# The weight block of the fourth leading unit's second product, loaded and rounded before the sums of unit 0

## The chip, the cores and the metric

The kernel runs on one core of one Trainium2 chip. The metric is the device time of one execution in microseconds (us). Times here are the median of several executions; the profile is one further execution, taken by the hardware profiler.

The engines are PE (TensorE: matrix products), ACT (ScalarE), DVE (VectorE), POOL (GpSimd, which here mainly issues adding transfers) and SP (SyncE, which issues plain transfers). Each has an instruction stream of its own and waits on semaphores for the others.

## What is computed

A trunk of two layers over 512 tokens of width 1024 in float32. Each layer is a token mixer and a SwiGLU channel mixer, each followed by a residual sum and a layer norm:

```python
for i in range(DEPTH):                      # DEPTH = 2
    m = diff_attention(h, ...) if i % 2 == 0 else short_gated_conv(h, ...)
    h = layer_norm(ALPHA * h + m, ln1_g[i], ln1_b[i])
    h = layer_norm(ALPHA * h + swiglu(h, w_gate[i], w_up[i], w_down[i]), ln2_g[i], ln2_b[i])

def swiglu(x, w_gate, w_up, w_down):        # w_gate, w_up: 1024 x 2816; w_down: 2816 x 1024
    return (silu(x @ w_gate) * (x @ w_up)) @ w_down
```

The change lies in the gate and up products of SwiGLU, once in each layer.

## The kernel before

**Precision.** PE multiplies float32 values in a rounded form (F32R). Every factor is therefore split into a rounded `hi` and a rest `lo`, and a product is three matmuls: hi·hi, hi·lo, lo·hi. The split of a plain weight block is `plain` (line 171): two ACT instructions write `hi` (L173) and the negated copy `lo` (L174), and then POOL issues a transfer that adds the raw block onto `lo` (L175). The split of a computed value is `split` (L57 on ACT for `hi`, then L58 on DVE for `lo`).

**Units and blocks.** The 2816 hidden columns fall into 11 units of 256. For each unit the gate and the up weights are cut into 2x2 blocks named "11", "12", "21", "22" (512 KB each). A unit is computed as seven block products in the manner of Strassen and Winograd, on sums of weight blocks (`t1` to `t4`, L611 on DVE) and on sums of activation blocks (`s1` to `s4`). The products of one unit in order are: x11 with block 11 (`start`), x12 with block 21 (`second`, into the same bank `x`), then `rest`: s2 with t2 into a bank `y`, s1 with t1 into a bank `z`, s3 with t3 added onto `y`, s4 with block 22 added onto `z`, and x22 with t4 added onto `y`. One product is 24 matmuls of 128x128 weights and 256 columns, all on line 623. Before `y` is added to, DVE must have read it (`u2`, L663); before `z` is added to, DVE must have read it (`w5`, L667).

**Leading units.** At the start of each SwiGLU the activations of tokens 256 to 511 are not ready. So the first four units (LEAD = 4) do their `start` and `second` products first; these need only tokens 0 to 255. Meanwhile ACT and DVE form s1 to s4 and x22 for the other tokens (`turn_forms`, lines 231 to 243) in two pieces, `soon` and `later`. `next21(u)` loads block 21 of unit u and splits it by `plain`. `sums(0, ...)` computes t1 and t2 of unit 0.

**Buffers.** Blocks 11 and 22, and block 21 of the leading units, go through three buffers tagged `raw`; blocks 12 and 21 of the rest go through two buffers tagged `raw2`. Blocks 12 and 22 of unit 0 are loaded into these two by hand. Block 21 of unit 0, called `raw_0_21` below, therefore waits until `t3` has read block 12; and block 12 of unit 1, `raw_1_12`, waits until `t4` has read `raw_0_21`. On SP the load of `raw_0_21` stands behind that of block 11 of unit 2, which waits for the adding transfer of the fourth leading unit's block 21.

**Order.** The recording layer orders each engine's instructions by the position in the program and by a plan of its own for when operands are ready; an engine then runs its stream strictly in that order. ACT's stream is therefore not the order of the source lines.

Of the kernel before, what the change touches and what calls it, by code (L numbers as in the profile page):

```python
# [39 lines left out]
def trunk(ctx: ExitStack, tc: tile.TileContext, t: dict):  # L40
# [4 lines left out]
    wpool = ctx.enter_context(tc.tile_pool(name="wpool", bufs=6))  # L45
# [4 lines left out]
    def bank(name):  # L50
        return psum.tile([P, 512], F32, tag="ps", name=name)
# [49 lines left out]
    def slot(pool, tag, shape, dt, name):  # L101
        return pool.tile([P, *shape], dt, tag=tag, name=name)
# [56 lines left out]
    def load_gu(i, u, key, pool, tag, n):  # L159
        a, b = int(key[0]) - 1, int(key[1]) - 1  # L160
        raw = pool.tile([P, 4, 256], F32, tag=tag, name=f"raw_gu{i}_{u}_{key}", bufs=n)
        nc.sync.dma_start(raw, t["wgu"][i, u, a, b])
        return raw

    def pair_gu(name):
        hi = wpool.tile([P, 4, 256], F32R, tag="whi", name=f"whi_{name}")
        lo = wpool.tile([P, 4, 256], F32R, tag="wlo", name=f"wlo_{name}")
        return hi, lo


    def plain(raw, name, pair=None):
        hi, lo = pair or pair_gu(name)
        nc.scalar.copy(hi, raw)  # L173
        nc.scalar.activation(lo, raw, AF.Copy, scale=-1.0)  # L174
        nc.gpsimd.dma_start(lo, raw, accum_op=ALU.add)  # L175
        return hi, lo
# [14 lines left out]
    lead = {}  # L191
# [399 lines left out]
    def swiglu(i, x, turns, open_next, out):  # L591
# [3 lines left out]
        with ExitStack() as fctx:  # L595
            wk = fctx.enter_context(tc.tile_pool(name=f"gu{i}", bufs=1, reuse_waits="tile"))

            def blocks(u, keys):
                return {
                    key: load_gu(i, u, key, *((wpool, "raw", 3) if key[0] == key[1] else (wk, "raw2", 2)))  # L600
                    for key in keys
                }

            def combined(raw, name):
                hi, lo = pair_gu(name)
                split(hi, lo, raw)
                return hi, lo
# [7 lines left out]
            def product(ps, w, key, first):  # L615
                xh, xl = x[key]
                for f in range(2):
                    o = ps[:, f * HALF : (f + 1) * HALF]
                    fs = slice(f * P, (f + 1) * P)
                    for k in range(4):  # L620
                        wh, wl = w[0][:, k, fs], w[1][:, k, fs]
                        for n, (a, b) in enumerate(((wh, xh), (wh, xl), (wl, xh))):
                            nc.tensor.matmul(o, a, b[:, k, :], start=first and f + k + n == 0,  # L623
                                             stop=k == 3 and n == 2, skip_group_check=True)

            def temp(tag, u, bufs=1):
                return wk.tile([P, 512], F32, tag=tag, name=f"{tag}{i}_{u}", bufs=bufs)
# [5 lines left out]
            def start(u, w):  # L633
                s = {"x": bank(f"x{i}_{u}")}
                product(s["x"], w, "x11", True)
                if u < 3:
                    both = slot(slots["xa"], f"h{UNITS - 5 - u}", (2, 512), F32, f"lead{i}_{u}")
                    s["e"], s["g"] = both[:, 0, :], both[:, 1, :]
                else:
                    s["e"], s["g"] = temp("e", u, 2), temp("g", u)  # L640
                return s

            def keep(s):
                nc.scalar.copy(s["e"], s["x"])
# [5 lines left out]
            def sums(u, raw):  # L650
                nm = f"gu{i}_{u}_"
                t1 = tsum(raw["12"], raw["11"], ALU.subtract, nm + "t1")
                t2 = tsum(raw["22"], t1, ALU.subtract, nm + "t2")
                return t1, t2, combined(t2, nm + "t2")
# [33 lines left out]
            def next21(u):  # L688
                return plain(load_gu(i, u, "21", wpool, "raw", 3), f"gu{i}_{u}_21")

            state, w2, later = [], [], []
            state.append(start(0, lead[i][0]))
            w2.append(next21(0))
            keep(state[0])
            soon = turns[0]()
            w2.append(next21(1))
# [1 line left out]
            later.append(soon[1])  # L698
            state.append(start(1, lead[i][1]))
            keep(state[1])  # L700
            soon = turns[1]()
            for u in range(2, LEAD):
                state.append(start(u, lead[i][u]))
            soon[0]()
            later.append(soon[1])
            raw = load_gu(i, 2, "21", wpool, "raw", 3)
            raw0 = {key: load_gu(i, 0, key, wk, "raw2", 2) for key in ("12", "22")}
            raw0.update(blocks(0, ("11",)))
            keep(state[2])
            w2.append(plain(raw, f"gu{i}_2_21"))  # L710
            keep(state[3])
            tw = sums(0, raw0)
            w2.append(next21(3))
            t1w = combined(tw[0], f"gu{i}_0_t1")
            for f in later:
                f()
# [4 lines left out]
            for u in range(1, UNITS):  # L721
                raw = blocks(u, ("11", "12", "22", "21"))
# [27 lines left out]
    def open_conv():  # L750
        slots["c"] = right_pool("x2")
        return new_xT(slots["c"], "x2")

    xT2, turns = swiglu(0, xT1, turns, open_conv, None)


    with ExitStack() as cctx:
# [42 lines left out]
        for ct in range(2, KD):  # L800
# [9 lines left out]
                             fetch=lambda: fetch_gu(1))  # L810

    swiglu(1, xT3, turns, lambda: None, t["out"])
    slots.pop("f").release()

# [51 lines left out]
```

## Time and profile before

| What | Value |
|---|---|
| Executions without profile | 1133.21, 1133.42, 1137.79 us |
| Median | 1133.42 us |
| The profiled execution | 1137.3 us |
| Span in its trace, first to last instruction | 1135.5 us (1.8 us lie around it) |
| PE busy | 1113.9 us, 98% |
| DVE busy | 736.3 us, 65% |
| ACT busy | 522.1 us, 46% |
| POOL busy | 118.6 us, 10% |
| Mean granted TensorE clock | 0.997 of full |
| HBM traffic | 119.81 MB read, 2.10 MB written |

PE carries the time: it is busy for all but some 22 us of the span, so a change of other engines' work shows in the time where PE waits, or comes to wait. The stretches of the change are the beginnings of the two SwiGLU blocks, near 250 to 290 us and 780 to 820 us. The three runs without profile spread over 4.6 us, and the profiled execution stands at the upper end of that spread.

### The profile page before, as it was taken

How to read it: one execution, taken by the hardware profiler on the slowest of the kernel's cores; microseconds unless marked ns; L12 is line 12 of the kernel's file. 1: busy time of each engine (PE TensorE's matmuls, PEld its weight loads, DVE VectorE, ACT ScalarE, POOL GpSimd, SP SyncE). 2: the span in 40 equal slices, each digit the busy share in tenths (PEclk: the TensorE clock that was granted, in tenths of full speed). 3: DMA queues.
4: the chain of work that ended last, by engine and by line, in shares of the span. 5: the costliest groups of instructions: out<-in, count | busy, mean ns of one | idle time of the engine just before them, and what ended most of it. 6: DMA issues, size and time to landing. Idle time of an engine off the chain costs nothing.

```text
span 1135.5 us, 17877 instructions
## 1 busy us (share of the span) xinstructions
PE 1113.9 (98%) x7242; PEld 994.1 (88%) x7242; DVE 736.3 (65%) x1065; ACT 522.1 (46%) x790; POOL 118.6 (10%) x149
## 2 busy tenths in 40 slices
PE   9999999999999999999999999999899999999997
PEld 6877887788999999988889888889899999988886
DVE  6777877587996776823355544448798767672416
ACT  5555555656455565711212432235555565651210
POOL 1111112140011111000010000013001111100002
PEclk9999999999999999999999999999999999999999
DMA  8521212278678777533313433377777877753302
GB/s 271 199 77 38 75 57 83 68 171 244 195 189 191 191 176 186 133 109 93 111 56 112 148 93 93 96 182 168 205 195 198 183 178 185 158 149 93 110 21 74
DMA packets 45315, 157.68 MB, mean 139 GB/s; under 512 B 5264, under 2 KB 6160, under 8 KB 45232
## 3 DMA queue, kind: packets, MB, share of 16 engines
q1 hardware_dynamic: 35728, 121.93, 34.7%
q0 software_dynamic: 9504, 34.61, 16.8%
q8 instruction: 57, 0.93, 0.3%
q14 instruction: 26, 0.21, 0.1%
HBM read 119.81 MB, written 2.10 MB: 107 GB/s over the span
## 4 chain that ended last, share of the span: by engine, by line
PE 73%; DVE 11%; DMA 5%; issue 4%; ACT 4%; POOL 2%; SPq 0%; POOLq 0%; DVEq 0%; ACTq 0%
PE y L623 14%; PE z L623 9%; PE x L623 7%; PE o_dn L77 7%; PE o_dn L76 7%; PE o_dn L75 7%; PE in L75 4%; PE in L77 4%; PE in L76 4%; DMA raw_gu<-in_wgu 3%; DMA wlo_gu<-raw_gu 2%; ACT p L476 1%; DVE nm L473 1%; DVE gu_t L611 1%; PE o_wo L75 1%
## 5 line engine op out<-in xcount | busy, mean ns | idle before, releaser
L57 ACT CAST whi_gu_t<-gu_t 128x1024 fp32r<-128x1024 f32 x88 | 91.1, 1049 | 82.0 <-DVE gu_t L611 40.5
L58 DVE TENSOR_TENSOR wlo_gu_t<-gu_t,whi_gu_t 128x1024 fp32r<-128x1024 f32 x88 | 107.1, 1223 | 30.0 <-ACT whi_gu_t L57 30.0
L58 DVE TENSOR_TENSOR wlo_dn<-raw_dn,whi_dn 128x1024 fp32r<-128x1024 f32 x44 | 53.6, 1223 | 112.5 <-ACT whi_dn L57 112.4
L75 PE MATMUL o_dn<-whi_dn,hid 128*128 128x512 f32 (+1 forms) x320 | 123.8, 387 | 0.0
L77 PE MATMUL o_dn<-whi_dn,hid 128*128 128x512 f32 (+1 forms) x320 | 123.8, 387 | 0.0
L76 PE MATMUL o_dn<-wlo_dn,hid 128*128 128x512 f32 (+1 forms) x320 | 123.8, 387 | 0.0
L57 ACT CAST whi_dn<-raw_dn 128x1024 fp32r<-128x1024 f32 x44 | 46.1, 1052 | 141.0 <-PE o_dn L77 107.5
L623 PE MATMUL x<-x_x_hi,wlo_gu 128*128 128x256 f32 x352 | 99.3, 282 | 4.3 <-DMA wlo_gu<-raw_gu 4.3
L175 POOL DMA_DIRECT2D wlo_gu<-raw_gu x66 | 57.5, 871 | 437.1 <-ACT wlo_gu L174 368.8
L623 PE MATMUL y<-x_s_hi,whi_gu_t 128*128 128x256 f32 x352 | 98.9, 281 | 1.3 <-DVE u L663 1.3
L623 PE MATMUL x<-x_x_hi,whi_gu 128*128 128x256 f32 x352 | 99.4, 282 | 0.0
L623 PE MATMUL x<-x_x_lo,whi_gu 128*128 128x256 f32 x352 | 98.9, 281 | 0.0
L623 PE MATMUL y<-x_s_hi,wlo_gu_t 128*128 128x256 f32 x352 | 98.3, 279 | 0.0
L623 PE MATMUL y<-x_s_lo,whi_gu_t 128*128 128x256 f32 x352 | 98.2, 279 | 0.0
L173 ACT CAST whi_gu<-raw_gu 128x1024 fp32r<-128x1024 f32 x66 | 69.0, 1050 | 61.3 <-PE y L623 30.7
L75 PE MATMUL in<-x_hi,whi_in 128*128 128x512 f32 (+1 forms) x240 | 83.7, 349 | 0.0
L77 PE MATMUL in<-x_hi,wlo_in 128*128 128x512 f32 (+1 forms) x240 | 83.2, 347 | 0.0
L76 PE MATMUL in<-x_lo,whi_in 128*128 128x512 f32 (+1 forms) x240 | 82.8, 345 | 0.0
L174 ACT ACTIVATE wlo_gu<-raw_gu 128x1024 fp32r<-128x1024 f32 x66 | 69.7, 1055 | 7.5 <-PE o_wco L76 6.0
L76 PEld LDWEIGHTS o_dn<-wlo_dn,hid 128*128 128x128 f32 x320 | 60.2, 188 | 13.1
L77 PEld LDWEIGHTS o_dn<-whi_dn,hid 128*128 128x128 f32 x320 | 60.1, 188 | 13.0
L75 PEld LDWEIGHTS o_dn<-whi_dn,hid 128*128 128x128 f32 x320 | 60.2, 188 | 13.0
(237 smaller groups left out, 3115.8 us busy)
## 6 DMA issues: line engine op xcount, KB each, us to landing
raw_gu<-in_wgu SPq DMA_DIRECT2D x104, 512.0 KB, 4.6
wlo_gu<-raw_gu POOLq DMA_DIRECT2D x66, 512.0 KB, 5.9
raw_dn<-in_wdn SPq DMA_DIRECT2D x44, 512.0 KB, 3.6
raw_in<-in_win SPq DMA_DIRECT2D x24, 512.0 KB, 3.6
raw_qk<-in_wqk SPq DMA_DIRECT2D x14, 512.0 KB, 3.9
raw_v<-in_wv SPq DMA_DIRECT2D x8, 512.0 KB, 5.5
raw_wo<-in_wo SPq DMA_DIRECT2D x8, 512.0 KB, 3.6
raw_wco<-in_wco SPq DMA_DIRECT2D x8, 512.0 KB, 3.8
```

The lines of the kernel that those rows point to most:

```text
L57: nc.scalar.copy(hi, src)
L58: nc.vector.tensor_tensor(lo, src, hi.bitcast(F32), op=ALU.subtract)
L75: nc.tensor.matmul(out, lh, rh, start=first, stop=False)
L76: nc.tensor.matmul(out, lh, rl, start=False, stop=False)
L77: nc.tensor.matmul(out, ll, rh, start=False, stop=last)
L173: nc.scalar.copy(hi, raw)
L174: nc.scalar.activation(lo, raw, AF.Copy, scale=-1.0)
L175: nc.gpsimd.dma_start(lo, raw, accum_op=ALU.add)
L473: nc.vector.tensor_reduce(nm, ps[c][:, :n], axis=AX.X, op=ALU.max, negate=True)
L476: nc.scalar.activation(pc[:, :n], ps[c][:, :n], AF.Exp, bias=nm, accum_out=sm)
L611: nc.vector.tensor_tensor(r, a, b, op=op)
L623: nc.tensor.matmul(o, a, b[:, k, :], start=first and f + k + n == 0, stop=k == 3 and n == 2, skip_group_check=True)
```

## The change

Block 21 of the fourth leading unit (u = 3) is loaded and split by `plain` in the place where that of the third (u = 2) stood, ahead of `sums(0, ...)`; before, it stood behind it. The block of the third unit moves up to just behind `keep(state[1])`. The number of instructions, loads and bytes stays the same.

```diff
-            state, w2, later = [], [], []
-            state.append(start(0, lead[i][0]))
-            w2.append(next21(0))
+            state, later = [start(0, lead[i][0])], []
+            w2 = [next21(0)]
...
             state.append(start(1, lead[i][1]))
             keep(state[1])
+            w2.append(next21(2))
             soon = turns[1]()
             for u in range(2, LEAD):
                 state.append(start(u, lead[i][u]))
             soon[0]()
             later.append(soon[1])
-            raw = load_gu(i, 2, "21", wpool, "raw", 3)
             raw0 = {key: load_gu(i, 0, key, wk, "raw2", 2) for key in ("12", "22")}
             raw0.update(blocks(0, ("11",)))
+            raw = load_gu(i, 3, "21", wpool, "raw", 3)
             keep(state[2])
-            w2.append(plain(raw, f"gu{i}_2_21"))
+            w2.append(plain(raw, f"gu{i}_3_21"))
             keep(state[3])
             tw = sums(0, raw0)
-            w2.append(next21(3))
             t1w = combined(tw[0], f"gu{i}_0_t1")
```

The order of instructions on PE, on POOL and on SP is the same in both kernels, apart from buffer numbers. What moves is on ACT and DVE.

ACT, first layer, from the rounding of s2 for tokens 256 to 383 on. In the names, `gu0_3_21` is block 21 of the fourth unit, `gu0_0_t2` the sum t2 of unit 0, `x1_s1` to `x1_s4` and `x1_x22` the activation sums, `lead0_2` and `e0_3` the kept partial products. Before:

```order
L57 CAST x1_s2_hi_2679<-x1_raw_x11_2685 128x4x128
L57 CAST x1_s3_hi_2681<-x1_raw_s3_2688 128x4x128
L57 CAST x1_s1_hi_2675<-x1_raw_x21_2687 128x4x128
L57 CAST x1_x22_hi_2677<-tp_wo_3_1_3027 128x4x128
L644 COPY lead0_2_3057<-x0_2_3032 128x512
L57 CAST whi_gu0_0_t2_3112<-gu0_0_t2_3110 128x1024
L57 CAST x1_s2_hi_2679<-x1_raw_x11_2685 128x4x128
L173 CAST whi_gu0_3_21_3118<-raw_gu0_3_21_3116 128x1024
L644 COPY e0_3_3083<-x0_3_3058 128x512
L174 ACTIVATE wlo_gu0_3_21_3119<-raw_gu0_3_21_3116 128x1024
L57 CAST whi_gu0_0_t1_3123<-gu0_0_t1_3108 128x1024
```

After the change, from the same instruction on:

```order
L57 CAST x1_s2_hi_2679<-x1_raw_x11_2685 128x4x128
L173 CAST whi_gu0_3_21_3109<-raw_gu0_3_21_3106 128x1024
L174 ACTIVATE wlo_gu0_3_21_3110<-raw_gu0_3_21_3106 128x1024
L57 CAST x1_s1_hi_2675<-x1_raw_x21_2687 128x4x128
L644 COPY lead0_2_3064<-x0_2_3039 128x512
L57 CAST whi_gu0_0_t2_3119<-gu0_0_t2_3117 128x1024
L57 CAST x1_s2_hi_2679<-x1_raw_x11_2685 128x4x128
L57 CAST whi_gu0_0_t1_3123<-gu0_0_t1_3115 128x1024
L644 COPY e0_3_3090<-x0_3_3065 128x512
L57 CAST x1_s3_hi_2681<-x1_raw_s3_2688 128x4x128
L57 CAST x1_x22_hi_2677<-tp_wo_3_1_3034 128x4x128
```

The two instructions of `gu0_3_21` move up past the roundings of s3, s1, x22, s2 and t2.

DVE, first layer, from the sum behind t2 (s2 for tokens 384 to 511) to t3. Before:

```order
L234 TENSOR_TENSOR x1_raw_x11_2685<-x1_raw_x21_2687,x1_raw_x11_2685 128x4x128
L58 TENSOR_TENSOR x1_s1_lo_2676<-x1_raw_x21_2687,x1_s1_hi_2675 128x4x128
L58 TENSOR_TENSOR x1_s3_lo_2682<-x1_raw_s3_2688,x1_s3_hi_2681 128x4x128
L58 TENSOR_TENSOR wlo_gu0_0_t2_3113<-gu0_0_t2_3110,whi_gu0_0_t2_3112 128x1024
...
L58 TENSOR_TENSOR x1_s4_lo_2684<-x1_raw_x12_2686,x1_s4_hi_2683 128x4x128
L58 TENSOR_TENSOR x1_x22_lo_2678<-tp_wo_3_1_3027,x1_x22_hi_2677 128x4x128
L241 TENSOR_TENSOR x1_raw_x12_2686<-x1_raw_x12_2686,x1_raw_x11_2685 128x4x128
L611 TENSOR_TENSOR gu0_0_t3_3297<-raw_gu0_0_22_3097,raw_gu0_0_12_3095 128x1024
```

After the change, the same stretch:

```order
L234 TENSOR_TENSOR x1_raw_x11_2685<-x1_raw_x21_2687,x1_raw_x11_2685 128x4x128
L58 TENSOR_TENSOR x1_s1_lo_2676<-x1_raw_x21_2687,x1_s1_hi_2675 128x4x128
L58 TENSOR_TENSOR wlo_gu0_0_t2_3120<-gu0_0_t2_3117,whi_gu0_0_t2_3119 128x1024
L58 TENSOR_TENSOR x1_s2_lo_2680<-x1_raw_x11_2685,x1_s2_hi_2679 128x4x128
L58 TENSOR_TENSOR wlo_gu0_0_t1_3124<-gu0_0_t1_3115,whi_gu0_0_t1_3123 128x1024
...
L58 TENSOR_TENSOR x1_x22_lo_2678<-tp_wo_3_1_3034,x1_x22_hi_2677 128x4x128
L241 TENSOR_TENSOR x1_raw_x12_2686<-x1_raw_x12_2686,x1_raw_x11_2685 128x4x128
L611 TENSOR_TENSOR gu0_0_t3_3297<-raw_gu0_0_22_3102,raw_gu0_0_12_3100 128x1024
```

On DVE the rests of t2 and t1 stand further forward, and of s4's first rest only the place changes: ahead of t3 before, behind it now. In the second layer both engines' streams move in the same way, except that there s4's first rest stays ahead of t3.

## Rows read from the trace of the kernel before

**Rows 1.** The page, first part: busy time and share of PE.

```profile
PE 1113.9 (98%) x7242; PEld 994.1 (88%) x7242; DVE 736.3 (65%) x1065; ACT 522.1 (46%) x790; POOL 118.6 (10%) x149
```

**Rows 2.** Waits of PE: total us, times, longest us.

```profile
PE x L623 <- DMA wlo_gu<-raw_gu: 4.3, 2, 2.8
```

**Rows 3.** Timeline of PE: start us, duration us, instruction, [idle before it, releaser].

```profile
274.99 0.38 PE L623 MATMUL x<-x_x_hi,wlo_gu 128*128 128x256 f32 x1 [2.77 <-DMA wlo_gu<-raw_gu]
...
288.60 0.35 PE L623 MATMUL z<-x_s_hi,whi_gu 128*128 128x256 f32 x1 [0.75 <-DVE w L667]
...
804.30 0.39 PE L623 MATMUL x<-x_x_hi,wlo_gu 128*128 128x256 f32 x1 [1.56 <-DMA wlo_gu<-raw_gu]
...
813.88 0.36 PE L623 MATMUL y<-x_s_hi,whi_gu_t 128*128 128x256 f32 x1 [1.06 <-DVE u L663]
...
817.75 0.36 PE L623 MATMUL z<-x_s_hi,whi_gu 128*128 128x256 f32 x1 [0.81 <-DVE w L667]
```

**Rows 4.** Critical chain in both stretches: start us, duration us, what.

```profile
255.71 10.63 DMA raw_gu<-in_wgu
...
270.05 4.89 DMA wlo_gu<-raw_gu
...
787.33 7.67 DMA raw_gu<-in_wgu
...
798.82 5.44 DMA wlo_gu<-raw_gu
...
804.70 4.79 DMA raw_gu<-in_wgu
...
810.76 3.74 DMA raw_gu<-in_wgu
```

**Rows 5.** Timeline of ACT in both stretches, columns as in rows 3.

```profile
261.80 0.62 ACT L57 CAST x_s_hi<-x_raw_x 128x512 fp32r<-128x512 f32 x1 [2.79 <-DVE x_raw_x L234]
...
265.73 1.06 ACT L57 CAST whi_gu_t<-gu_t 128x1024 fp32r<-128x1024 f32 x1
266.69 0.61 ACT L57 CAST x_s_hi<-x_raw_x 128x512 fp32r<-128x512 f32 x1
267.20 1.05 ACT L173 CAST whi_gu<-raw_gu 128x1024 fp32r<-128x1024 f32 x1
268.16 0.57 ACT L644 COPY e<-x 128x512 f32<-128x512 f32 x1
268.63 1.06 ACT L174 ACTIVATE wlo_gu<-raw_gu 128x1024 fp32r<-128x1024 f32 x1
...
790.60 0.62 ACT L57 CAST x_s_hi<-x_raw_x 128x512 fp32r<-128x512 f32 x1 [1.08 <-DVE x_raw_x L234]
```

**Rows 6.** Timeline of DVE in both stretches, columns as in rows 3.

```profile
266.21 0.68 DVE L58 TENSOR_TENSOR x_s_lo<-x_raw_x,x_s_hi 128x512 fp32r<-128x512 f32 x1
266.81 0.68 DVE L58 TENSOR_TENSOR x_s_lo<-x_raw_s,x_s_hi 128x512 fp32r<-128x512 f32 x1
...
273.89 1.22 DVE L611 TENSOR_TENSOR gu_t<-raw_gu,raw_gu 128x1024 f32<-128x1024 f32 x1
...
802.37 1.22 DVE L611 TENSOR_TENSOR gu_t<-raw_gu,raw_gu 128x1024 f32<-128x1024 f32 x1
```

**Rows 7.** SP's load at 275.42; times to landing near 275.4 (two loads) and 281.2.

```profile
275.42 0.38 SPq L162 DMA_DIRECT2D raw_gu<-in_wgu  x1
...
DMA to landing us min/median/max: 3.6/4.1/4.5
...
DMA to landing us min/median/max: 4.2/4.2/4.2
```

**Rows 8.** Stretches: us, busy us (instructions) of PE, PEld, DVE, ACT, POOL; PEclk, DMA share, GB/s.

```profile
267.00:270.00 3.00, 3.00 (x29) 3.00 (x28) 3.00 (x5) 3.00 (x5) 0.00 (x0) 1.00 0.97 381
275.00:279.00 4.00, 4.00 (x21) 4.00 (x22) 1.94 (x3) 3.44 (x4) 0.01 (x1) 0.57 0.74 249
805.00:809.00 4.00, 4.00 (x36) 4.00 (x35) 0.98 (x1) 2.71 (x4) 0.85 (x1) 1.00 0.85 271
```

## The prediction

> **What bounds the kernel now.** I read the page's busy times first: PE is busy for 1113.9 of 1135.5 us [rows 1], so time can be won or lost only where PE waits. The table of PE's waits names the place the change aims at: the `second` products stop twice, once in each layer, for the adding transfer of a `lo` block, 4.3 us in all [rows 2]. PE's timeline gives the two, 2.77 us before 274.99 and 1.56 us before 804.30, and behind them smaller ones of another kind [rows 3]: `z` waits 0.75 us at 288.60 for DVE's `w5`; in the second layer `y` waits 1.06 us at 813.88 for `u2` and `z` 0.81 us at 817.75 for `w5`. These follow the aimed-at wait by some 14 us, and they decide what its removal is worth.
>
> The chain of waits shows why ACT was late with this block: its load was issued at 255.71 and landed 10.63 us later, at 266.34; in the second layer it was issued at 787.33 and landed after 7.67 us, at 795.00 [rows 4]. ACT rounded the block at 267.20 [rows 5], 0.86 us after the landing, so its old place in ACT's stream fits the arrival almost exactly. In the meantime ACT rounded s3, s1, x22 and t2, which DVE waits for. DVE has no air there: 3.00 of 3.00 us busy from 267 to 270 [rows 8].
>
> **The change part by part.**
>
> *The loads.* SP's order is the same in both kernels, and nothing ahead of this load moves on any engine. So the block is not loaded earlier. It lands near 266.3 and 795.0 as before.
>
> *The third unit's block.* It stands in the same place on ACT, POOL and SP: no cost. The new order also swaps one pair of `hi`/`lo` buffers between t2 and the moved block; t2 now takes the pair of unit 0's first product, which PE left before 255, so it does not wait.
>
> *ACT.* The two instructions now stand right behind the cast that begins at 261.80 [rows 5]. ACT finishes that at 262.4 and then waits for the landing at 266.34: 3.9 us of waiting where it used to round for DVE. From there I count with the spacing of the rows [rows 5]: a 1024-wide instruction 0.96 us (265.73 to 266.69, 267.20 to 268.16), a 512-wide cast 0.51 (266.69 to 267.20), a copy 0.47 (268.16 to 268.63). Block 21: `hi` 266.37, `lo` 267.33, ended 268.39. Then s1 at 268.29, ended 268.91; the copy 268.80; t2 269.28, ended 270.34; s2 270.24; t1 270.75, ended 271.80; the copy 271.71; s3 272.2; x22 272.7.
>
> *What that gives PE at the aimed-at wait.* `lo` ended at 269.69 before (268.63 and 1.06) and the adding transfer started at 270.05, 0.36 us behind, landing 4.89 us later [rows 4, 5]. Now it starts at 268.75 and lands at 273.64: 1.3 us of the 2.77 are saved in the first layer. In the second the same count from 795.00 gives a `lo` end at 797.05, an issue at 797.4 and, with the 5.44 us of [rows 4], a landing at 802.9: 1.4 of the 1.56 us.
>
> *What it costs DVE.* The rest of s1 started at 266.21 before [rows 6]. Now it needs the cast that ends at 268.91. DVE starts it at 268.94, needs 0.60 (266.21 to 266.81 [rows 6]), waits until 270.37 for t2, and then runs without a gap: rest of t2 (1.13), s2 (0.60), rest of t1 (1.14), then s3, x22, the sum for s4, and the same three again, 0.60 each. t3 starts at 276.84 and ends at 278.06. It started at 273.89 before [rows 6]: 2.95 us later. That is 2.7 for s1 and 0.8 for t2, less 0.6 for the rest of s4 that now stands behind t3. In the second layer this rest stays ahead of t3; t3 ends 12.3 us behind the landing instead of 11.7, at 807.3 instead of 803.6 (802.37 and 1.22 [rows 6]).
>
> *Who waits for t3.* The load of `raw_0_21` takes the buffer that t3 frees; t4 needs it; `raw_1_12` takes the buffer that t4 frees; DVE's t1 and t2 of unit 1 need that and stand ahead of `w5`; and PE's s4 product waits for `w5`. Before, `raw_0_21` was issued at 275.42 [rows 7] and at 804.70 [rows 4]; now at 278.1 and 807.35, **2.7 us later** in each layer. The adding transfer that held SP before, landing at 274.94 (270.05 and 4.89 [rows 4]), no longer does.
>
> *The two transfers of that chain* are the unknown. `raw_0_21` took 4.5 us beside the load issued just ahead of it, which took 3.6 [rows 7], and 4.8 us in the second layer [rows 4]. Now that neighbour has landed before it starts. I take 3.6 us: 0.9 and 1.2 us back. The ends are the old durations (nothing back) and 3.5. `raw_1_12` took 4.2 us [rows 7] and 3.7 us [rows 4]; it now lies wholly beside the adding transfer of block 22, which t3 also delays, where it did so for 2.6 and 1.3 us before. I take 4.6 us in both, 0.4 and 0.9 more; the ends are nothing more, and the 4.8 us of the longest load, 0.6 and 1.1 more.
>
> *Sum.* First layer 2.7 − 0.9 + 0.4 = 2.2 us, second 2.7 − 1.2 + 0.9 = 2.4 us: **4.6 us longer**. The 1.3 and 1.4 us won at the aimed-at wait are not subtracted: PE gets through it earlier and then stands longer before `y` and `z`, because DVE sets when the s4 product starts (288.60 and 817.75 [rows 3]). From there the rest runs as before. With the ends of the transfers the sum is 3.1 (1.0 and 1.3 us back, nothing given) to 7.1 us (nothing back, 0.6 and 1.1 given).
>
> The Trainium skill (DMA: Bandwidth & Descriptors, "Anatomy of one DMA — SWDGE (gpsimd) path") gives 2.0 us and the bytes over 436 GB/s for a transfer that GpSimd issues, an estimate of 3.2 us for 512 KB; with that for `raw_0_21` the sum would be 3.8 us. None of the loads in [rows 7] is that short, and the sum goes by these.
>
> Against its own time the profiled execution would go from 1137.3 to 1141.9 us. It stands 3.9 us above the median of 1133.42, and no row here tells why. I put the sum on the median, which two of three runs share: **1138.0 us**, 0.4% longer.
>
> **The rivals.**
>
> *The clock falls too (clearly slower).* Before the s3 product PE will wait until `u2`, which stands behind the rest of t4 on DVE: t4 ends near 282.9, its cast at 284.1, its rest at 285.3, `u2` at 286.0, while PE is through with s1 by 282 to 283 (273.7 and three products of some 2.9 us). That is a wait of 3 to 4 us. After the 2.77 us wait the granted clock was 0.57 of full from 275 to 279, mostly the lower of its levels, 1.2 GHz; after the wait of 1.56 us it was 1.00 from 805 to 809 [rows 8]. PE got through 21 matmuls in the one stretch and 36 in the other, so a low stretch costs 4 x (1 − 21/36) = 1.7 us. In the forecast this is hidden, since the s3 product still ends before `w5`. It decides once the low stretch reaches into the s4 product: 1.7 us in each layer, 8.0 us in all, 1141.4 us.
> The Trainium skill (TensorE: Matmul & The Clock Gate, "What's actually happening") says that an idle array is put to half its clock; by that rule the new wait costs this again, and the trace agrees after the wait of 2.77 us and not after that of 1.56.
>
> *The block lands in time (no change, or a shade faster).* If ACT did not have to wait, t3 would come no later. Even then little is won: `raw_0_21` cannot be issued before t3 ends, at 275.1 against 275.42, and at 803.6 against 804.70, so 0.3 and 1.1 us, 1.4 us in all: 1132.0 us. It decides if the load takes 4 us less than 10.63 and 7.67 [rows 4]. SP's queue gives no reason for that.
>
> *The aimed-at wait is worth its price (faster).* To be faster by over 0.5%, 5.7 us, PE would have to lose almost all of its five waits, 6.95 us [rows 3]; 4.3 us gone alone would give 1129.1. Against it stands the chain behind t3.
>
> **How the numbers follow.** The chances: forecast 0.62 (3.1 to 7.1 us, so 1136.5 to 1140.5), clock 0.18 (6.5 to 10.5 us, 1139.9 to 1143.9), landing in time 0.16, faster 0.04. The range holds the forecast whole and the clock case to 1143.0; below, it goes somewhat over halfway to the landing case, to 1134.6, since runs of one kernel scatter by 4.6 us. A measurement of this kernel can tell about 0.5%, 5.7 us, from no change. Slower by more is the clock case and a quarter of the forecast: 0.33. Within it: the rest of the forecast and the landing case, 0.63. Faster: 0.04.
>
> **What would show it.** ACT idle for some 4 us before L173 at 266.4 and 795.0, released by a DMA: the core of the argument; if ACT does not wait there, the forecast falls. PE's wait for `lo` at 1.4 us and at nearly nothing. t3 at 276.8 and 806.1. Two long waits of PE near 282 to 286 and 811 to 816 for `u2`, each followed by one for `w5`, with the s4 product at 290.8 and 820.1. PEclk below 1 behind 286 tells how near the clock case is. An s4 product at or before 288.6 would make the prediction wrong.

## The result

The changed kernel takes 1143.87 us (median of six executions, 1143.09 to 1146.15). The kernel before, on the same chip beside it, took 1137.64 (six executions). The ratio is 1.0059 with a 95% interval of 1.0044 to 1.0075 (further ratios and intervals below are to the kernel before, in the same way): the change makes the kernel **0.6% slower, some 6 us**. The forecast was 4.6 us, put on 1133.42, with a range that ends at 1143.0; the time lies above it.

The profiled execution went from a span of 1135.5 to 1141.9 us. PE's waits in the changed kernel, in total us, times, longest (before: [rows 2]):

```profile
PE z L623 <- DVE w L667: 4.5, 2, 2.8
PE x L623 <- DMA wlo_gu<-raw_gu: 4.0, 2, 2.9
PE y L623 <- DVE u L663: 3.1, 2, 2.5
```

PE's timeline at the same places as in [rows 3]:

```profile
275.90 0.39 PE L623 MATMUL x<-x_x_hi,wlo_gu 128*128 128x256 f32 x1 [2.85 <-DMA wlo_gu<-raw_gu]
...
286.55 0.36 PE L623 MATMUL y<-x_s_hi,whi_gu_t 128*128 128x256 f32 x1 [0.61 <-DVE u L663]
...
291.28 0.36 PE L623 MATMUL z<-x_s_hi,whi_gu 128*128 128x256 f32 x1 [1.67 <-DVE w L667]
...
806.58 0.39 PE L623 MATMUL x<-x_x_hi,wlo_gu 128*128 128x256 f32 x1 [1.17 <-DMA wlo_gu<-raw_gu]
...
817.60 0.36 PE L623 MATMUL y<-x_s_hi,whi_gu_t 128*128 128x256 f32 x1 [2.50 <-DVE u L663]
...
823.50 0.55 PE L623 MATMUL z<-x_s_hi,whi_gu 128*128 128x256 f32 x1 [2.84 <-DVE w L667]
```

The aimed-at wait has hardly moved: 2.77 and 1.56 us before, 2.85 and 1.17 now. The waits for DVE's `u2` and `w5` behind it grew from 2.6 to 7.6 us. ACT shows where that begins:

```profile
266.60 1.05 ACT L173 CAST whi_gu<-raw_gu 128x1024 fp32r<-128x1024 f32 x1 [4.00 <-DMA raw_gu<-in_wgu]
...
797.36 1.05 ACT L173 CAST whi_gu<-raw_gu 128x1024 fp32r<-128x1024 f32 x1 [3.32 <-DMA raw_gu<-in_wgu]
```

And DVE shows how it goes on, with the rest of s1 and t3 (266.21, 273.89 and 802.37 in [rows 6]), and then with t1 of unit 1, which waits for `raw_1_12` and stands ahead of `w5`:

```profile
269.15 0.69 DVE L58 TENSOR_TENSOR x_s_lo<-x_raw_x,x_s_hi 128x512 fp32r<-128x512 f32 x1 [2.29 <-ACT x_s_hi L57]
...
277.06 1.22 DVE L611 TENSOR_TENSOR gu_t<-raw_gu,raw_gu 128x1024 f32<-128x1024 f32 x1
...
288.05 1.22 DVE L611 TENSOR_TENSOR gu_t<-raw_gu,raw_gu 128x1024 f32<-128x1024 f32 x1 [1.65 <-DMA raw_gu<-in_wgu]
...
808.43 1.22 DVE L611 TENSOR_TENSOR gu_t<-raw_gu,raw_gu 128x1024 f32<-128x1024 f32 x1
...
820.27 1.23 DVE L611 TENSOR_TENSOR gu_t<-raw_gu,raw_gu 128x1024 f32<-128x1024 f32 x1 [2.82 <-DMA raw_gu<-in_wgu]
```

The chain of waits has the two loads behind t3, `raw_0_21` and `raw_1_12`, and the s4 product at its end (start, duration; compare [rows 4, 7]):

```profile
278.30 3.86 DMA raw_gu<-in_wgu
...
283.44 4.59 DMA raw_gu<-in_wgu
...
291.28 3.07 PE z L623 x24
...
809.68 3.53 DMA raw_gu<-in_wgu
...
814.49 5.76 DMA raw_gu<-in_wgu
...
823.50 4.51 PE z L623 x24
```

To compare traces that begin with different offsets I take a span of each layer: from the last statistics of the layer norm ahead of the stretch (DVE, L123, at 252.16 and 782.68 before) to the first ones of the next norm (583.25 and 1112.38). All kernels of this study, in us; the layers are of the one profiled execution, the time is the median of all:

| Kernel | First layer | Second layer | Time, median |
|---|---|---|---|
| before | 331.09 | 329.70 | 1137.5 to 1137.8 |
| changed | 333.56 | 333.41 | 1143.87 |
| lo last, on before | 331.38 | 329.04 | 1137.16 |
| POOL splits the block, on changed | 337.77 | 333.77 | 1143.13 |
| t3 early, on changed | 335.87 | 333.11 | 1146.37 |
| t3 early, on before | 332.68 | 331.01 | 1140.54 |
| first layer only | 333.25 | 329.68 | 1139.72 |
| second layer only | 331.36 | 333.20 | 1141.28 |
| pins, on changed | 330.90 | 330.41 | 1138.47 |
| pins, on before | 329.25 | 326.97 | 1133.24 |
| pins and lo last, on changed | 330.89 | 329.83 | 1138.61 |
| pins and lo last, on before | 328.54 | 321.83 | 1132.53 |
| own buffer and pins, on changed | 332.05 | 332.15 | 1140.62 |
| own buffer and pins, on before | 331.73 | 330.76 | 1139.15 |

The change costs 2.5 us in the first layer and 3.7 in the second. Two profiled executions lie far from their medians: that with the POOL split took 1148.82 us, the slowest of its six, and that of pins and `lo` last on the kernel before 1126.88, the fastest of its twelve.

### The profile page after: what moved, and what is told of

The parts are those of the page before. It is cut to its first block, busy times and chain, and to the rows that moved or that the text cites. A ratio compares the mean times of both kernels' runs of the same rounds, so it can differ in the third digit from the quotient of the medians.

```text
span 1141.9 us, 17879 instructions
## 1 busy us (share of the span) xinstructions
PE 1115.6 (98%) x7242; PEld 996.1 (87%) x7242; DVE 736.5 (64%) x1065; ACT 522.5 (46%) x790; POOL 118.9 (10%) x149
## 4 chain that ended last, share of the span: by engine, by line
PE 75%; DVE 9%; DMA 5%; ACT 5%; issue 3%; POOL 2%; SPq 0%; POOLq 0%; DVEq 0%; ACTq 0%
PE y L623 15%; PE z L623 11%; PE x L623 7%; PE o_dn L76 7%; PE o_dn L77 7%; PE o_dn L75 7%; PE in L75 4%; PE in L77 4%; PE in L76 4%; DMA raw_gu<-in_wgu 4%; ACT p L476 1%; DVE nm L473 1%; PE o_wo L75 1%; PE o_wo L77 1%; PE o_wo L76 1%
```

## Experiments

**Is the aimed-at wait worth anything?** In the kernel before, the second product of the fourth unit does its eight matmuls with `lo` last, so PE needs the block later; ACT and DVE are untouched.

```diff
+            def lo_last(ps, w, key):
+                xh, xl = x[key]
+                for n in range(3):
+                    for f in range(2):
...
+                            a, b = ((w[0], xh), (w[0], xl), (w[1], xh))[n]
...
-                second(state[u], w2[u])
+                second(state[u], w2[u], u == LEAD - 1)
```

> The kernel before, but in the second product of the fourth unit PE does its eight matmuls with the lo block last, behind the sixteen with hi, so that it needs lo some 1.8 us later; nothing else is changed. This takes from PE's wait what the change wanted to take from it, without touching ACT and DVE. Theory (DVE's w5 sets the start of the s4 product, so PE's wait for lo is slack): the wait shrinks from 2.77 to about 1 us and from 1.56 to nothing, PE's waits for u2 and w5 grow by as much, and the time stays at 1137.6, within 1.5 us. Rival (the wait is worth its price): 3.3 us faster, 1134.3.

Ratio to before 1.0002 (0.9988 to 1.0016). PE's timeline:

```profile
274.62 1.21 PE L654 MATMUL x<-x_x_hi,wlo_gu 128*128 128x256 f32 x8 [1.62 <-DMA wlo_gu<-raw_gu]
...
283.86 0.38 PE L623 MATMUL y<-x_s_hi,whi_gu_t 128*128 128x256 f32 x1 [2.37 <-DVE u L677]
...
813.37 0.55 PE L623 MATMUL y<-x_s_hi,whi_gu_t 128*128 128x256 f32 x1 [2.97 <-DVE u L677]
```

Of 4.3 us of waiting for `lo` 1.6 are left. PE now waits 2.37 and 2.97 us for `u2` (L677 is L663 of this file), where it waited 0 and 1.06, and no longer for `w5` (0.75 and 0.81). In all it waits 6.96 us in these stretches, and 6.95 before. Nothing is won that these runs can show; the interval leaves room for some 1.4 us. A part of this is the clock: over the 4 us behind the two waits the granted clock was 0.57 and 0.61, and the s4 product began 0.4 and 0.7 us behind the end of `w5`, so an estimate from these rows is that at most some 1 us would have been won without the low clock.

**ACT without the wait.** The changed kernel; POOL makes `hi` and `lo` of the block.

```diff
-            w2.append(plain(raw, f"gu{i}_3_21"))
+            hi, lo = pair_gu(f"gu{i}_3_21")
+            nc.gpsimd.tensor_copy(hi, raw)
+            nc.gpsimd.tensor_scalar_mul(lo, raw, -1.0)
+            nc.gpsimd.dma_start(lo, raw, accum_op=ALU.add)
+            w2.append((hi, lo))
```

> The changed kernel, but the fourth unit's block 21 is split by two POOL instructions (copy, times -1) in place of the two on ACT. ACT then does not wait for this block's landing; PE gets its lo block later, since POOL is the slower engine (an estimate from POOL's 128x512 instructions of 1.35 to 1.46 us: some 2.8 us each). Theory (the price is ACT's wait, handed on to DVE, t3, the load of raw_0_21 and so to w5): ACT has no wait of 4.00 and 3.32 us any more, the rest of s1 starts near 266.5 instead of 269.15, t3 not later than 274.5 instead of 277.06, and the s4 product starts at or before 289.5 instead of 291.28. Time 1136 to 1140 us, though PE's wait for the lo block grows from 2.85 to 4.5 or more. Rival (what PE waits for at the adding transfer is the price): the time grows with that wait, to 1147 us or more.

1143.13 us, ratio 1.0053 (1.0037 to 1.0070): neither side (the rows are of the slowest execution, 1148.82 us). ACT's wait is gone and t3 starts at 274.21, as expected. But POOL took 4.96 and 3.11 us where I had estimated 2.8 each, and the adding transfer landed only at 279.24. The load of `raw_0_21` stands on SP behind the load that waits for this transfer. DVE's row for t4:

```profile
287.38 1.23 DVE L611 TENSOR_TENSOR gu_t<-raw_gu,gu_t 128x1024 f32<-128x1024 f32 x1 [9.57 <-DMA raw_gu<-in_wgu]
```

So `raw_0_21` has two gates, t3 and the adding transfer, and the later one counts. The experiment only changed the gate and doesn't tell the theories apart.

**t3 earlier.** t3 is computed right behind `sums(0, raw0)`, in both kernels.

```diff
             tw = sums(0, raw0)
+            t3 = tsum(raw0["22"], raw0["12"], ALU.subtract, f"gu{i}_0_t3")
```

> The changed kernel, but DVE computes t3 of unit 0 right behind the rest of s2, where t3's two blocks have long landed, and no longer behind the rests of s3, x22 and s4. ACT waits for the landing as in the changed kernel. Theory (the late t3 holds the load of raw_0_21 back): t3 starts near 272.5 instead of 277.06, and raw_0_21 is then issued when SP is free of the block in front of it, near 276.3 and 807.0 instead of 278.30 and 809.68; the s4 product starts 1 to 2 us earlier in each layer; time 1139 to 1141.5 us against 1143.9. Rival (ACT's and DVE's delay of the activation sums is the price by itself, whatever t3 does): 1143.9 us, no difference.

> The kernel before, with the same edit: t3 of unit 0 right behind the rest of s1. Theory: in the kernel before the load of raw_0_21 is held by SP, which waits for the adding transfer of the fourth unit's block 21 (landing 274.94 and 804.26), not by t3 (ended 275.11 and 803.59); so an earlier t3 moves that load by 0.3 us at most and the time stays at 1137.6, within 1.5 us. If t3 were the limit in the kernel before too, 1 to 3 us would be won.

Both missed: 1146.37 us (ratio 1.0075, 1.0062 to 1.0088) and 1140.54 (1.0019, 1.0002 to 1.0037). t3 did move, to 272.10 in the changed kernel, but the recording layer's plan (the planner) then put t1 of unit 1 ahead of `u2` of unit 0. DVE and PE there:

```profile
287.47 1.23 DVE L611 TENSOR_TENSOR gu_t<-raw_gu,raw_gu 128x1024 f32<-128x1024 f32 x1 [3.54 <-DMA raw_gu<-in_wgu]
...
289.44 0.55 PE L623 MATMUL y<-x_s_hi,whi_gu_t 128*128 128x256 f32 x1 [5.92 <-DVE u L663]
```

`u2` now stands behind an instruction that waits for `raw_1_12`, and PE waits 5.92 us for it. In the kernel before the same edit makes PE wait 1.44 us for `u2` at 287.77, but the larger part of its loss is another: SP now loads `raw_0_21` ahead of block 11 of unit 2, at 268.42 in place of 275.42, and the adding transfer beside it takes 6.06 and 8.45 us in place of 4.89 and 5.44. PE waits 4.40 and 4.74 us for `lo`, and in the second layer for nothing else:

```profile
808.97 0.54 PE L623 MATMUL x<-x_x_hi,wlo_gu 128*128 128x256 f32 x1 [4.74 <-DMA wlo_gu<-raw_gu]
```

An edit that the planner answers with another order tests that order; the pins below fix the order.

**Layer by layer.** The change in one layer (`i == 0`, or `i == 1`), the old lines in the other.

```diff
+            if i == 0:
...
+                raw = load_gu(i, 3, "21", wpool, "raw", 3)
...
+            else:
...
+                w2.append(next21(3))
```

> The change in the first layer only. From the last statistics of the layer norm ahead of the stretch to the first ones of the next norm the trace of before takes 331.09 us in the first layer and 329.70 in the second, the changed kernel 333.56 and 333.41, so 2.5 and 3.7 us more. Theory (each layer's price is its own): 333.5 in the first and 329.7 in the second layer, 1140.2 us in all.

> The change in the second layer only. Forecast for this layer was 2.4 us; the changed kernel showed 3.7, with raw_1_12 at 5.76 us in place of 4.6 and a low clock in the s4 product. Theory: the second layer's price does not come from the first layer's delay; 331.1 and 333 to 333.5 us, 1141 us in all. If the long transfer of raw_1_12 was chance, it takes 4.6 us here and the second layer 332.1.

1139.72 us (ratio 1.0025, 1.0007 to 1.0042) and 1141.28 (1.0033, 1.0019 to 1.0048), with the spans as expected: each layer pays its own price, and the layer with the old lines comes out within 0.3 us of before. The chain of the second, in its second layer:

```profile
808.78 3.42 DMA raw_gu<-in_wgu
...
813.49 5.84 DMA raw_gu<-in_wgu
...
822.58 3.06 PE z L623 x24
```

In the second layer `raw_1_12` takes 5.84 us here, 5.76 in the changed kernel and 5.90 with the pins below (813.69), against 3.74 before [rows 4] and 3.62 with the change in the first layer only. It was not chance. The clock can be told apart in part. Stretches behind the wait for `w5` of the changed kernel and, below it, of the one changed in the second layer only (us; busy us of PE, PEld, DVE, ACT, POOL; PEclk, DMA share, GB/s):

```profile
823.00:825.00 2.00, 1.50 (x7) 1.53 (x8) 2.00 (x3) 2.00 (x3) 0.00 (x0) 0.58 0.57 225
```

```profile
823.00:825.00 2.00, 2.00 (x19) 2.00 (x18) 2.00 (x3) 2.00 (x3) 0.00 (x0) 1.00 0.75 195
```

The granted clock was 0.58 in one and 1.00 in the other, and the s4 product took 4.51 and 3.06 us, yet the layer's span is 333.41 and 333.20. So the low clock is not the main price. It is not nothing either: in the kernel changed in the second layer only the s4 product began 3.52 us later than before and the span is 3.50 longer, while in the changed kernel it began 3.08 later (counted from the statistics) and the span is 3.7 longer. The low stretch first put the next product 4.5 us behind, and most of that was made good in the units that follow; some 0.6 us of the 3.7, an estimate from these starts, came with the clock.

**The last link of the chain.** Two places in DVE's stream are pinned: t4's rest behind `u2`, and all DVE work of unit 1 behind the first `w5` of unit 0. (`issue_after` queues what a block of the program records on an engine behind a given instruction of that engine; it orders and doesn't wait.) ACT's and PE's streams around the place stay.

```diff
-                v(u2, s["e"], y, op=ALU.add)
+                first = v(u2, s["e"], y, op=ALU.add)
...
+                with tc.issue_after(first.ins) if u == 0 else ExitStack():
+                    w = combined(t4, nm + "t4")
-                product(y, combined(t4, nm + "t4"), "x22", False)
+                product(y, w, "x22", False)
...
+                    with tc.issue_after(state[0]["w5"].ins) if u == 1 else ExitStack():
+                        tw = sums(u, raw)
+                        rest(u, state[u], raw, tw, False)
```

> The changed kernel with two places in DVE's stream pinned: u2 of unit 0 stands directly behind t4 (ahead of t4's rest), and w5 of unit 0 stands ahead of t1 and t2 of unit 1, so that it no longer waits behind them for raw_1_12. ACT's stream, the loads and PE's stream around the place stay as in the changed kernel: ACT still waits some 4 and 3.3 us for the landing, t3 and raw_0_21 stay as late. Theory (the late t3 costs time only over raw_0_21 and raw_1_12, which DVE waits for ahead of u2 and w5): PE's waits for u2 and w5 (7.6 us in the changed kernel) shrink to under 1.5 us and the time falls from 1143.9 to 1135.5 to 1138 us; of the 6.2 us between the two kernels at most 2 stay against the kernel before with the same pins. Rival (the delay of the activation sums on ACT and DVE is a price by itself): over 1141 us, and over 4 us behind the kernel before with the same pins.

> The kernel before with the same two pins. Its waits for u2 and w5 are 0.75, 1.06 and 0.81 us. Theory: they go, 2.6 us, 1134 to 1136 us; PE's wait for the lo block (2.77 and 1.56 us) stays and is now what PE waits for in the stretch.

By the medians the pins are worth 5.4 us in the changed kernel (1138.47; ratio to before 1.0022, 1.0005 to 1.0039) and 4.6 in the kernel before (1133.24; 0.9968, 0.9949 to 0.9988), more than the 2.6 us of its waits. That PE's waits for `u2` and `w5` go, held. That at most 2 us stay between the two kernels did not: 5.2 stay, as the rival had it, 1.65 in the first layer and 3.44 in the second. PE's rows, changed with pins and then before with pins:

```profile
276.71 0.45 PE L623 MATMUL x<-x_x_hi,wlo_gu 128*128 128x256 f32 x1 [2.71 <-DMA wlo_gu<-raw_gu]
...
805.97 0.58 PE L623 MATMUL x<-x_x_hi,wlo_gu 128*128 128x256 f32 x1 [2.08 <-DMA wlo_gu<-raw_gu]
...
822.85 0.35 PE L623 MATMUL y<-x_x_hi,whi_gu_t 128*128 128x256 f32 x1 [1.19 <-DVE w L672]
```

```profile
274.55 0.38 PE L623 MATMUL x<-x_x_hi,wlo_gu 128*128 128x256 f32 x1 [2.74 <-DMA wlo_gu<-raw_gu]
...
802.79 0.39 PE L623 MATMUL x<-x_x_hi,wlo_gu 128*128 128x256 f32 x1 [2.30 <-DMA wlo_gu<-raw_gu]
```

The third row shows a part of it: I had cut the chain at `w5`'s first use only. Its second one (L672, ahead of the x22 product) still stands behind t1 and t2 of unit 1, and so behind `raw_1_12`, which is still late. At the x22 product this makes 1.35 of the 3.44 us. Another 1.14 us are there before, at the s2 product, though `lo` lands 0.4 us earlier: from 806 to 810 the changed kernel's granted clock was 0.58, over the 4 us at the same place in the kernel before 1.00. The first layer has no such wait; its s4 product begins 0.5 us later, and the rest of its 1.65 us builds up over the next units in steps too small for the profile to name a cause. So these two runs don't decide whether the delay of the activation sums costs something by itself.

**Both at once.** The two kernels with pins, and `lo` last as above.

> The changed kernel with both pins and with the fourth unit's lo matmuls last, so that PE needs the lo block some 1.8 us later. Theory: with the chain behind t3 cut off, a shorter wait for lo is worth its time, other than in the kernel before alone: 1.5 to 3 us less than the changed kernel with pins, 1133 to 1136 us, less where u2 (behind t4, which raw_0_21 sets) stops PE instead. If the wait for lo is worth nothing even here, the time equals that of the changed kernel with pins.

> The kernel before with both pins and the fourth unit's lo matmuls last. The same edit of the order of matmuls alone gave a ratio of 1.0002 on the kernel before. Theory: with the pins it is worth 2 to 3.3 us: 1131 to 1133.5 us, 4 to 6 us under the kernel before. If PE's waits at this place are worth nothing, it equals the kernel before with pins.

1138.61 us (1.0018, 1.0000 to 1.0036) on the changed kernel, nothing won, where I expected 1.5 to 3; 1132.53 (0.9967, 0.9947 to 0.9987) on the kernel before, 0.7 us where I expected 2 to 3.3. In the changed kernel PE's 2.03 us at 283.42 and 1.21 at 812.32 for `u2` took the place of the waits for `lo`: `u2` stands behind t4, and t4 waits for `raw_0_21`. In the second layer PE waits 1.63 us more, at 820.46, for `w5`'s second use. The two versions of the kernel before with pins are the only ones here whose interval lies below the kernel before, by some 0.3%.

**The chain cut at its head.** On top of the pins, `raw_0_21` gets a buffer of its own, so that it waits for neither t3 nor the adding transfer, and `raw_1_12` waits for t3 and not for t4.

```diff
-            raw0.update(blocks(0, ("21",)))
+            raw0["21"] = slot(slots["xb"], "h3", (4, 256), F32, f"raw_gu{i}_0_21")
+            nc.sync.dma_start(raw0["21"], t["wgu"][i, 0, 1, 0])
```

> The changed kernel with both pins, and raw_0_21 is loaded into a buffer of its own, ahead of block 11 of unit 2 on SP: it waits for nothing any more, and raw_1_12 then waits for t3 and not for t4. ACT waits for the landing of the fourth unit's block 21 and DVE's t3 comes late, as in the changed kernel. Theory (the price is that late t3 makes raw_1_12 late, and with it DVE's t1 and t2 of unit 1, for which DVE, busy all the time from there on, has no time to spare): raw_1_12 lands near 282.5 instead of 288.0, DVE makes good its lost 3 us where it used to wait for raw_0_21, and of the difference of 5.2 us between the two kernels with pins at most 2 stay against the kernel before with the same edits: 1133.5 to 1136 us. Rival (ACT's wait and the late activation sums cost by themselves): 1138 us as with the pins alone, over 4 us behind the kernel before with the same edits.

> The kernel before with both pins and raw_0_21 in a buffer of its own. In the kernel before with pins PE waits for nothing in the stretch but the lo block (2.7 and 2.3 us) any more. Theory: little left to win, 1132 to 1134 us against its 1133.2.

1140.62 us (1.0042, 1.0024 to 1.0059) and 1139.15 (1.0025, 1.0011 to 1.0039): the difference between the two kernels has shrunk from 5.2 to 1.5 us, as the theory forecast. The times themselves missed, both by some 5 us. DVE in the changed kernel, t4 and `u2`:

```profile
280.21 1.22 DVE L611 TENSOR_TENSOR gu_t<-raw_gu,gu_t 128x1024 f32<-128x1024 f32 x1
284.77 0.69 DVE L663 TENSOR_TENSOR u<-lead,y 128x512 f32<-128x512 f32 x1 [3.34 <-PE y L623]
```

Here DVE waits for no load any more; it waits for PE. ACT's wait is still there, the rest of s1 begins at 268.78 and t3 at 276.68. What PE waits for is the adding transfer, in the chain of the changed and then of the kernel before:

```profile
268.60 8.49 DMA wlo_gu<-raw_gu
```

```profile
270.57 6.01 DMA wlo_gu<-raw_gu
```

Moved forward, `raw_0_21` runs beside this transfer, which took 4.89 us before [rows 4]. PE now stands 4.45 and 4.65 us in the first layer, with a low clock behind it (0.50 and 0.63 over 4 us), and no DVE chain hides that. What is left of the difference arises here. Counted from the statistics, the s2 product of the changed kernel starts 1.1 us later in the first layer and 1.0 in the second than in the kernel before with the same edits; `lo` lands 0.5 and 1.0 us later, and in the first layer the lower clock does the rest. Behind it PE waits for nothing that ACT's and DVE's delay makes late. This doesn't refute the rival by itself, since PE comes later here and a delay of DVE can hide behind that. DVE waits 3.34 us for PE at `u2`, and the s2 product starts 2.33 us later than in the changed kernel with pins alone; by these rows, an estimate, some 1 us of room would be left to DVE without the longer transfer.

## Why the prediction was wrong, and where it was right

*The mechanism* of the chain was right. ACT waits 4.00 and 3.32 us for the landing; t3 starts at 277.06 (forecast 276.84; 0.2 us of offset lie ahead of the stretch); `raw_0_21` is issued 2.7 us later in the first layer, counted from the statistics (25.94 against 23.26), and 2.3 in the second (24.32 against 22.02). The s4 product starts 2.5 and 3.1 us later, and with the change in one layer alone only that layer gets longer. That it is `raw_0_21` and `raw_1_12` that carry the price is read from the chain of waits; the experiments support it (5.2 us of difference with pins, 1.5 with the chain cut at its head), but none of them isolates it. That the gain at `lo` was rightly not subtracted fits the experiment with `lo` last, where 2.7 us less of that wait won nothing clear of noise. The two long waits for `u2`, put at 3 to 4 us, came out at 0.61 and 2.50: PE was through with the s1 product only at 285.9, where I had counted 282 to 283, since it gained nothing at `lo`.

*The base* is the larger part of the miss. The step that failed is the last one of the sum, to put 4.6 us on the median of three runs, 1133.42. Six runs beside the result and 23 to 35 beside the experiments give the kernel before medians of 1137.5 to 1137.8; they reach from 1129.5 to 1140.9. Of the 5.9 us between forecast and result 4.2 are this; the other 1.7 are the change itself, 6.2 us for 4.6.

*The term of `raw_1_12` in the second layer* was mis-sized: 4.6 us, measured 5.76, 5.84 and 5.90. I had read its neighbour, the adding transfer of block 22, only as a small surcharge. In the first layer the same term was right to the hundredth (4.59), which is luck: in other executions with the change it took 4.22 to 5.21. `raw_0_21` took 3.86 and 3.53 us for 3.6. The Trainium skill's figure for a transfer that GpSimd issues (DMA: Bandwidth & Descriptors, "Anatomy of one DMA — SWDGE (gpsimd) path"), an estimate of 3.2 us for 512 KB, is met neither by these loads, which SP issues, nor by the adding transfers of block 22 in the changed kernel, which GpSimd issues (5.04 and 5.46 us).

Start of the s4 product, second layer, counted from the statistics: 2.30 (issue) − 1.26 (`raw_0_21`, from 4.79 to 3.53) + 2.02 (`raw_1_12`, from 3.74 to 5.76) = 3.06 us later; forecast 2.4. First layer: 2.68 − 0.64 + 0.39 = 2.43; forecast 2.2. The starts read from PE's timeline are 3.08 and 2.48 later. The 0.6 us by which the second layer's 3.7 exceeds 3.1 are the estimate for the clock above.

*The gain at the aimed-at wait* was wrong but not in the sum. I expected 1.4 us left of 2.77; there are 2.85. Counted from the statistics, POOL issued the adding transfer 1.3 us earlier, at 268.96, but it landed at 275.86, after 6.89 us and not 4.89, and so 0.7 us later than before. PE itself came to this place 0.6 us later in the first layer, where it now also waits for ACT's late copy of `lead0_2` (0.17 us before 269.65). The row for the long transfer was there: the DMA share was 0.97 from 267 to 270 [rows 8]. In the changed kernel the same stretch reads:

```profile
267.00:270.00 3.00, 2.83 (x25) 2.63 (x25) 0.69 (x1) 3.00 (x5) 0.88 (x1) 1.00 0.93 365
```

All the packets in it belong to plain loads. Issued 1.3 us earlier into queues this full, the transfer landed no earlier.

*The clock rival* came true only in part. Behind the waits for `u2`, where I had put it, the granted clock stayed at 1.00; in the second layer it fell behind the wait for `w5` (PEclk 0.58, mostly the lower level, 1.2 GHz), and an estimated 0.6 us of its price stayed, not 1.7 in each layer. The Trainium skill's rule that an idle array loses its clock (TensorE: Matmul & The Clock Gate, "What's actually happening") fits this fall. That none came in the kernel changed in the second layer only, behind a wait as long, 2.92 us, is not against it, as the page has the moment depend on a window that runs free of the kernel. *The block lands in time* is refuted, since ACT waited. *Worth its price* is refuted by the sign of the result.

What stays open: how much of the 0.4 us by which `raw_1_12` is slowed in the first layer, and of the 2.0 in the second, is its neighbour's. It lay beside the adding transfer of block 22 for 3.2 us in the one (that ran from 281.67 for 5.0 us) and for 4.5 in the other (from 813.53 for 5.5); no run takes that transfer away. A chain cut without the longer adding transfer was not tried, and whether the late activation sums cost something by themselves stays open with it.

## To carry to other kernels

An instruction that is moved up in a strictly ordered stream, to ahead of the landing of its operand, makes everything behind it wait; follow that through buffers to the next load, since a late reader is a late load. Before you shorten a wait, ask what the waiting engine would meet next: here taking 2.7 us from PE's wait won nothing clear of noise, since other waits grew by as much. When the few runs of a base fall into two groups, measure it more often before you put a sum on it, or let the range hold the sum on both. The profiled execution alone is no safer base: it happened to be near the median here, but it was the slowest of its runs in one version and the fastest in another.

## What the hardware showed that was not expected

PE showed two paces at full granted clock. The kernel before with pins, and then with pins and `lo` last, over the same stretches:

```profile
900.00:920.00 20.00, 20.00 (x173) 20.00 (x172) 13.64 (x15) 11.51 (x13) 2.59 (x3) 1.00 0.81 188
940.00:960.00 20.00, 20.00 (x172) 20.00 (x171) 15.37 (x18) 11.51 (x13) 2.60 (x3) 1.00 0.78 185
```

```profile
900.00:920.00 20.00, 20.00 (x179) 20.00 (x179) 15.53 (x17) 12.50 (x15) 2.59 (x3) 1.00 0.86 191
940.00:960.00 20.00, 20.00 (x179) 20.00 (x179) 13.99 (x15) 11.53 (x13) 3.41 (x4) 1.00 0.82 194
```

PEclk reads 1.00 in all four, and PE is busy throughout, but there are 172 or 173 matmuls in one and 179 in the other: their starts lie 117.8 and 113.3 ns apart. The second execution kept that pace from about 870 to 995 us and gained some 5 us by it. Its time, 1126.88 us, is the lowest of its kernel, whose others took 1131.2 to 1135.0; so its second layer in the table is not typical. The changed kernel with pins ran at this pace too, from about 880 to 940 us, so its second layer is also not free of it. That the scatter of the kernel before, 1129.5 to 1140.9 us, has the same cause fits in size and is not shown.

After waits of nearly one length the clock behaved differently: behind 2.84 us (changed) and 2.97 us (`lo` last) the granted clock was at its low level at once, behind 2.92 us (second layer only) it stayed at 1.00.
